# A hybrid stick-breaking / RWKV-7 layer on one core: the opening's loads, norm and gain spread rebuilt, V's projection called later, the sampled state update in full shape

## The chip, the core and the metric

One NeuronCore of a Trainium2 chip runs the whole layer in one launch. The metric is device time in microseconds (us). Engines are named as in the profile: PE (matmul), PEld (its weight loads), DVE (vector), ACT (scalar), POOL (GpSimd), SP (the queue that issues most DMAs).

## The reference

For 512 prompt tokens of one stream and 16 new tokens of each of 8 running streams (640 rows of width 1024, one layer), cut to what matters:

```python
h = rmsnorm(x, norm_g)                    # x * rsqrt(mean(x*x)) * norm_g
proj = h @ w_in                           # one projection: q,k,v,z_A | gates | r,k,v,w-lora,a-lora,z_B
o_a = stick_breaking_attention(q, k, v)   # 16 heads x 64
p_mix = p_b + mu_shift * (p_prev - p_b)   # token shift on the RWKV columns
S_t = S_{t-1} (diag(w_t) - kk_t^T (kk_t*a_t)) + v_t^T k_t ;  o_t = S_t r_t   # 16 heads x 64
y_a = (o_a * silu(z_a)) @ w_o_a ;  y_b = (groupnorm(o_b) + bonus) * silu(z_b) @ w_o_b
x + (sig(g_a)*y_a + sig(g_b)*y_b) @ w_out # then a final RMSNorm; k, v, shift rows and states go out too
```

## The kernel before

**Opening** (`start`, `late`). The 640 rows are five tiles x of 128 rows. Each is squared and summed on ACT (`square`), its 1/rms made by small DVE steps and a square root on ACT (`rstd`), scaled on DVE by 1/rms and by `gb`, the gain norm_g spread over all partitions (`scale`), transposed on PE into two banks, copied as fp32r into `xh` by ACT, with the rest `xl` taken by DVE (`put`). Tiles 3 and 4 lie in `x34`; `late` transposes them in the middle of the first product. `warm(n)` issues n idle products of a zero tile `wz`.

**Products** (`gemm_range`). A job is 128 columns of a projection: its weights `raw` come by DMA, ACT rounds them to `whi`, DVE takes the rest `wlo`, and PE adds, for eight k and two halves of the rows, xh·whi + xl·whi + xh·wlo: 48 products of some 320 columns. ps_g banks hold the results.

**Order.** The program is written out by a planner. `Driver.run` keeps generators (streams) and the main line of jobs; at each `yield` it looks at a model of the engines' clocks (`Clock`) and steps the first stream that the model calls ready, else the main line, which can also be held by a gate. Jobs come from three lists (`job`): `mixed` (R, K, V, in that order for each of 8 head pairs p, first come first served), `free` (q, k, v, z, gate A: the filling, spilled to DRAM as `sp`, and z_B after each V) and `later`. The head of `mixed` is called two jobs before it runs, when its `soon` is true or no filling is left; its gate can then still hold the main line.

**The recurrence of a pair.** `prep(p)` makes decay, keys and masks from R and K (its low-rank weights `wd` are split into `wh`, `wl`), `prep2` inverts small triangles on POOL, `samp` and `chain` run the steps, `sstate` (started from the first chain step) updates the eight sampled streams' states, `post` norms the result. V(p) writes over the buffer that `post(p-3)` still reads, so V's gate is `post(p-3)`. When the last post is done the attention streams open, with the remaining jobs as filling; then come the output products.

In `sstate` the tile `ux` holds, per group g of four streams, the last step's values masked by stream; products with `BKt` give the update, DVE adds the old state `S0T` into `sn`, POOL scales `sn`, PE transposes it.

Of the kernel before, what the change touches and what calls it, by code (L numbers as in the profile page):

```python
# [340 lines left out]
def body(tc, ins, outs, dbg=None):  # L341
# [157 lines left out]
    def gemm_range(i0, i1):  # L499
# [6 lines left out]
        for i in range(i0, i1):  # L506
# [59 lines left out]
    def start():  # L566
        x34 = pers.tile([128, 2, D], F32, tag="H", name="x34")
        srow = pers.tile([88, 3, 128], F32, tag="V", name="srow", bufs=3)
        with pool("start", bufs=1) as sp:
            xt = [sp.tile([128, D], F32, tag="x", name="x", bufs=3) for _ in range(3)]  # L570
            xt += [x34[:, 0], x34[:, 1]]

            def loadx(i):
                dma(out=xt[i], in_=ins["x_prompt"][0, i * 128:(i + 1) * 128, :] if i < 4 else
                    ins["x_sample"].rearrange("b t d -> (b t) d"))
            gb = sp.tile([128, D], F32, name="gb")
            wz = sp.tile([128, 512], BF16, name="wz")
            V.memset(wz, 0.0)
            psw = bank("g")

# [9 lines left out]
            dma(out=ident, in_=ins["consts"][:, 0:128])  # L590
            loadx(2)
            wload(0)
            loadx(3)
            loadx(4)
            prow = sp.tile([97, 128], F32, name="prow")
# [8 lines left out]
            dma(out=cst[:, 128:NC], in_=ins["consts"][:, 128:NC])  # L604
            sv = sp.tile([128, 5], F32, name="sv")
            sr = sp.tile([128, 5], F32, name="sr")
            st = sp.tile([128, 5], F32, name="st")
            junk = sp.tile([128, D], F32, name="junk")
# [4 lines left out]
            def rstd(i0, i1):  # L613
                c = slice(i0, i1)
# [8 lines left out]

            def pscale(i):
                G.tensor_scalar(out=xt[i], in0=xt[i], scalar1=sr[:, i:i + 1], scalar2=1.0, op0=ALU.mult, op1=ALU.mult)
                gtt(xt[i], xt[i], gb, ALU.mult)
# [84 lines left out]
    def rwkv_load(p):  # L711
        o = rw[p]
        wd = o["wd"] = tr.tile([128, 2, 128], F32, tag="wd", name="wd")
        for r, n in enumerate(("w2", "a2")):
            for half in range(2):
                dma(out=wd[RS[half], r, :], in_=ins[n][0, :, p * 128:(p + 1) * 128])

    def state_load(p):
        o = rw[p]
# [8 lines left out]
    def prep(p):  # L728
        yield flag("rkfree", p - 1) if p else flag("lat")
        o = rw[p]  # L730
        wd = o["wd"]
        yield [wd]
        wh = tr.tile([128, 2, 128], F32R, tag="wh", name="wh")
        wl = tr.tile([128, 2, 128], F32R, tag="wl", name="wl")
# [85 lines left out]
        rk = kkn  # L820
        stt(rk, R, pcol(RK, p), K, ALU.mult, ALU.mult)
        setf("rkfree", p)
        yield [H, BK]
# [270 lines left out]
    def sstate(p):  # L1094

        o = rw[p]
        X, BKt, S0T, wc = (o[n] for n in ("X", "BKt", "S0T", "wc"))
        psn = yield from take("b", X, hold=True)
        for g in range(2):
            uxs = [ch.tile([128, 4, 64], F32, tag="ux", name="ux", bufs=2) for _ in range(2)]  # L1100
            for h in range(2):
                gtt(uxs[h], X[:, 8 + g, h, :].unsqueeze(1).broadcast_to([128, 4, 64]),
                    cview["msk4"].unsqueeze(2).broadcast_to([128, 4, 64]), ALU.mult)
            yield uxs
# [3 lines left out]
        sn = ch.tile([128, 8, 64], F32, tag="sn", name="sn")  # L1108
        vtt(sn, psn.rearrange("p (b v) -> p b v", b=8), S0T, ALU.add)
        give(psn)  # L1110
        setf("schain", p)
# [15 lines left out]
    def post(p, S8):  # L1127
# [22 lines left out]
        tp(ps[0:64, 0:128], S8, ident)  # L1150
        so8 = ch.tile([64, 128], F32, tag="ux", name="so8", bufs=2)
        V.tensor_copy(so8, ps[0:64, 0:128])
# [269 lines left out]
    with tc.manual_schedule():  # L1422
# [91 lines left out]
        for p in range(NPAIR):  # L1514
# [224 lines left out]
        tr = tr_cm.__enter__()  # L1739
        G.memset(STG, 0.0)  # L1740
        for t in ABD:
            G.memset(t, 0.0)
        drv.run(program())
# [36 lines left out]
```

## Time and profile before

| what | value |
|---|---|
| median of 3 runs | 1173.54 us (1167.69 to 1175.17) |
| profiled execution | 1171.08 us, of which 1169.3 us span |
| granted PE clock over the span | 0.99 |
| DMA | 130.70 MB, mean 112 GB/s |

The span is what the trace covers; the execution is 1.78 us longer, and the profiled one lies 2.46 us under the median. The first 30 us are the opening, the recurrence with its jobs runs to about 775 us, the attention to about 1035 us, then come output products alone.

### The profile page before, as it was taken

To read this page: it belongs to the slowest core of one execution; us is meant where nothing else is said; L and a number is where in the kernel's file an instruction comes from. 1 tells how busy PE (TensorE), PEld (TensorE's weight loads), DVE (VectorE), ACT (ScalarE), POOL (GpSimd) and SP (SyncE) were. 2 spreads that over 40 slices of the span, in tenths; PEclk is the share of its full clock that TensorE was granted. 3 is DMA by queue.
4 is the path that set the end of the run, shared out by engine and by line. 5 is a ranking of instruction groups with operands and counts; after the bars stand their busy time and mean duration, and the time that the engine had idled before them with its cause. 6 is when DMAs were issued, how large, how long until landed. Compare 5 with 4: busy or idle time off the path is not lost. (4 is left out here: it accounts for less than half of the span.)

```text
span 1169.3 us, 25426 instructions
## 1 busy us (share of the span) xinstructions
PE 1111.5 (95%) x10050; PEld 1037.7 (89%) x10050; DVE 746.2 (64%) x1517; ACT 629.8 (54%) x1347; POOL 390.5 (33%) x605
## 2 busy tenths in 40 slices
PE   6999899989999999999899999999999989999997
PEld 4989899979989989889799899998888878899997
DVE  6485974847765867857767544337777688765424
ACT  5636357646666477466575556445555544522223
POOL 3033315125222243342342513034444454323302
PEclk9999999989999999999999999999999999999999
DMA  5222222213132232133132333369666676366312
GB/s 193 78 89 57 78 66 82 84 50 115 62 95 77 67 93 79 55 88 89 52 93 90 98 103 102 108 184 261 180 161 160 172 216 177 82 197 188 105 56 91
DMA packets 205294, 130.70 MB, mean 112 GB/s; under 512 B 78332, under 2 KB 184696, under 8 KB 205176
## 3 DMA queue, kind: packets, MB, share of 16 engines
q1 hardware_dynamic: 204888, 129.03, 37.8%
q8 instruction: 79, 1.29, 0.4%
q14 instruction: 39, 0.32, 0.1%
q0 software_dynamic: 288, 0.05, 0.0%
HBM read 97.70 MB, written 31.35 MB: 110 GB/s over the span
## 5 line engine op out<-in xcount | busy, mean ns | idle before, releaser
L213 PE MATMUL ps_g<-xh,whi 128*128 128x320 f32 (+1 forms) x1424 | 468.5, 329 | 1.7 <-ACT xh L213 1.3
L213 PE MATMUL ps_g<-xl,whi 128*128 128x320 f32 (+1 forms) x1424 | 443.5, 311 | 3.3 <-DVE xl L213 3.3
L213 PE MATMUL ps_g<-xh,wlo 128*128 128x320 f32 (+1 forms) x1424 | 443.0, 311 | 1.4 <-DVE wlo L213 1.4
L213 PEld LDWEIGHTS ps_g<-xh,whi 128*128 128x128 f32 x1424 | 271.4, 191 | 9.3 <-issue 3.0
L213 PEld LDWEIGHTS ps_g<-xl,whi 128*128 128x128 f32 x1424 | 270.9, 190 | 6.4 <-DVE xl L213 4.5
L213 PEld LDWEIGHTS ps_g<-xh,wlo 128*128 128x128 f32 x1424 | 270.0, 190 | 2.4 <-DVE wlo L213 2.4
L213 DVE TENSOR_TENSOR wlo<-raw,whi 128x1024 fp32r<-128x1024 f32 x97 | 123.6, 1274 | 69.6 <-ACT whi L213 69.0
L213 ACT ACTIVATE whi<-raw 128x1024 fp32r<-128x1024 f32 x97 | 102.7, 1059 | 48.6 <-DMA raw<-in_w_o_a_dram 28.6
L213 DVE TENSOR_TENSOR_SCAN kp<-kp,amsk 128x256 f32<-128x256 f32 (+3 forms) x80 | 73.6, 929 | 27.8 <-ACT kp L213 27.7
L213 POOL TENSOR_TENSOR bt<-bt,amsk 128x128 f32<-128x128 f32 x64 | 44.0, 691 | 124.3 <-ACT bt L213 81.5
L213 POOL TENSOR_TENSOR itmp<-INV 128x28 f32<-128x28 f32 (+6 forms) x112 | 47.0, 420 | 90.8 <-DVE INV L213 82.9
L213 ACT ACTIVATE kp<-ps_a 128x512 f32<-128x512 f32 (+3 forms) x72 | 33.1, 460 | 68.0 <-PE ps_a L213 42.2
L213 ACT ACTIVATE RH<-ps_b 128x128 f32<-128x128 f32 (+1 forms) x64 | 19.4, 302 | 77.8 <-PE ps_b L213 77.4
L213 ACT ACTIVATE sp<-ps_g 128x320 f32<-128x320 f32 x80 | 34.6, 437 | 45.9 <-PE ps_g L213 40.6
L213 ACT ACT_TABLE_LOAD x39 | 50.0, 1283 | 8.9 <-DVE BK L213 5.4
L213 DVE SCALAR_TENSOR_TENSOR X<-ps_b,wc,SW 64x64 f32<-64x64 f32 x96 | 26.7, 278 | 35.7 <-PE ps_b L213 34.9
L213 POOL TENSOR_TENSOR on<-on,V 128x640 f32<-128x640 f32 x8 | 12.4, 1550 | 108.9 <-ACT on L213 108.9
L213 DVE TENSOR_TENSOR bt<-bt,kp 128x511 f32<-128x511 f32 (+4 forms) x72 | 42.4, 588 | 7.7 <-POOL bt L213 0.3
L213 POOL TENSOR_TENSOR INV<-INV,itmp 128x28 f32<-128x28 f32 (+6 forms) x112 | 43.6, 390 | 8.8
L213 PE MATMUL ps_b<-cst,bt 128*128 128x128 f32 x192 | 33.5, 278 | 12.4 <-DVE bt L213 11.8
L213 PE MATMUL ps_g<-olo,mgh 128*128 128x256 f32 x160 | 45.0, 281 | 0.0
L213 PE MATMUL ps_g<-ohi,mgh 128*128 128x256 f32 x160 | 45.0, 281 | 0.0
(252 smaller groups left out, 2319.4 us busy)
## 6 DMA issues: line engine op xcount, KB each, us to landing
raw<-in_w_in_dram SPq DMA_DIRECT2D x81, 512.0 KB
q<-dr_q SPq DMA_DIRECT2D x32, 160.0 KB
Kr<-in_cache_sb_k_dram SPq DMA_DIRECT2D x16, 256.0 KB
Vp<-in_cache_sb_v_dram SPq DMA_DIRECT2D x16, 256.0 KB
raw<-in_w_o_b_dram SPq DMA_DIRECT2D x8, 512.0 KB
raw<-in_w_o_a_dram SPq DMA_DIRECT2D x8, 512.0 KB
oraw<-in_w_out_dram SPq DMA_DIRECT2D x4, 1024.0 KB
dr_zB<-zm SPq DMA_DIRECT2D x8, 320.0 KB
```

Of the source, the lines that this page charges most:

```text
L213: r = f(*a, **k)
```

## The change

- Opening: x and the other first loads are issued by SP and ACT in turn. norm_g comes as one row (`grow`) and PE spreads it: a column of ones times the row, two products of 512 columns, copied to `gb` by ACT. A square root on a dummy tile stands before them on ACT. Each tile is normed singly (before: 0; 1 and 2; 3 and 4). The low part of the first weights goes to POOL. The clearing of `STG` and of the two `AB` tiles on POOL comes in `late` (before: ahead of the jobs). Idle products: 6, 8, 4, 4, 4 (before 18, 6, 3).
- `gemm_range` yields after every k (before: every second).
- `rwkv_split(p+1)` splits the next pair's low-rank weights at the end of `prep(p)` (before: at the start of `prep(p+1)`).
- `sstate`: one product of 128x512 per group (before: two of 64x256 each), four DVE adds of 64x256 (before: one of 128x512), and the bank is not held over both groups.
- V(p) is called when `post(p-3)` is done (before: when `chain(p-3)` is).

```diff
@@ gemm_range
-                    if k % 2:
-                        yield
+                    yield
@@ start
+            ring = (nc.sync.dma_start, nc.scalar.dma_start)
             def loadx(i):
-                dma(out=xt[i], ...)
+                ring[i % 2](out=xt[i], ...)
+            V.memset(one, 1.0)
+            V.memset(sr, 1.0)
+            loadx(0)
+            ring[1](out=grow, in_=ins["norm_g"])
+            loadx(1)
+            ring[1](out=ident, in_=ins["consts"][:, 0:128])
+            loadx(2)
+            loadx(3)
+            wload(0)
+            loadx(4)
+            act(out=st, in_=sr, func=AF.Sqrt)
-            warm(18)
-            loadx(0)
-            dma(out=gb, in_=ins["norm_g"].partition_broadcast(128).rearrange("p o d -> p (o d)"))
-            loadx(1)
...
+            warm(6)
+            for hf in range(2):
+                ps = bank("g")
+                c = slice(hf * 512, hf * 512 + 512)
+                mm(ps, lhsT=one, rhs=grow[:, c], start=True, stop=True)
+                act(out=gb[:, c], in_=ps, func=AF.Copy)
+            warm(8)
...
             square(0)
-            rstd(0, 1)
+            rstd(0)
             scale(0)
             square(1)
-            square(2)
-            rstd(1, 3)
+            rstd(1)
             scale(1)
             put(0, xt[0], "ab")
-            warm(6)
+            warm(4)
+            square(2)
+            rstd(2)
+            scale(2)
             wsplit(0)
-            scale(2)
+            gtt(jobs[0].lo, jobs[0].raw, jobs[0].hi.bitcast(F32), ALU.subtract)
             put(1, xt[1], "ab")
-            warm(3)
-            wlow(0)
+            warm(4)
+            put(2, xt[2], "ab")
+            warm(4)
             square(3)
+            rstd(3)
+            scale(3)
             square(4)
-            put(2, xt[2], "ab")
-            warm(0)
-            rstd(3, 5)
+            rstd(4)
+            scale(4)
...
-            scale(3)
-            scale(4)
@@ late
+        for t in (STG, *ABD):
+            G.memset(t, 0.0)
@@ prep
-        yield [wd]
-        wh = ...; wl = ...
-        act(out=wh, in_=wd, func=AF.Copy)
-        yield [wh]
-        gtt(wl, wd, wh.bitcast(F32), ALU.subtract)
-        if p + 1 < NPAIR:
-            rwkv_load(p + 1)
+        if p == 0:
+            yield [o["wd"]]
+            rwkv_split(0)
...
+        if p + 1 < NPAIR:
+            rwkv_split(p + 1)
         setf("rkfree", p)
@@ sstate
+        sn = ch.tile([128, 8, 64], F32, tag="sn", name="sn")
         for g in range(2):
+            ux = ch.tile([128, 2, 4, 64], F32, tag="ux", name="ux")
             for h in range(2):
-                gtt(uxs[h], ...)
+                gtt(ux[:, h], ...)
-            for h in range(2):
-                mm(psn[RS[h], g * 256:(g + 1) * 256], lhsT=BKt[:, 8 + g, h * 64:(h + 1) * 64],
-                   rhs=uxs[h].rearrange("p b v -> p (b v)"), start=True, stop=True)
-        vtt(sn, psn.rearrange("p (b v) -> p b v", b=8), S0T, ALU.add)
+            ps = yield from take("b", ux)
+            mm(ps, lhsT=BKt[:, 8 + g, :], rhs=ux.rearrange("p h b v -> p (h b v)"), start=True, stop=True)
+            for h in range(2):
+                vtt(sn[RS[h], c], pv[RS[h], h], S0T[RS[h], c], ALU.add)
+            yield []
@@ program, jobs of pair p
-                g2, s2 = [("post", p - 3)], s2 + [("chain", p - 3)]
+                g2, s2 = [("post", p - 3)], s2 + [("post", p - 3)]
```

Where the instructions stand. First ACT, from its first instruction to the second tile's square root; `junk` is the square, `sr` the root, `x_105` the tile `x34`. Before:

```order
L213 ACT_TABLE_LOAD
L213 ACTIVATE junk,sv<-x 128x1024
L213 ACT_TABLE_LOAD
L213 ACTIVATE sr<-sv 128x1
L213 ACTIVATE junk,sv<-x 128x1024 x2
L213 ACTIVATE sr<-sv 128x2
```

and after:

```order
L589 DMA grow<-in_norm_g_dram 1x1024
L575 DMA x<-in_x_prompt_dram 128x1024
L591 DMA cst<-in_consts_dram 128x128
L575 DMA x_105<-in_x_prompt_dram 128x1024
L213 ACT_TABLE_LOAD
L213 ACTIVATE st<-sr 128x5
L213 ACTIVATE gb<-ps_g 128x512 x2
L213 ACTIVATE junk,sv<-x 128x1024
L213 ACTIVATE sr<-sv 128x1
L213 ACTIVATE junk,sv<-x 128x1024
L213 ACTIVATE sr<-sv 128x1
```

The second table load is gone from between the first square and its root; four DMA issues and two copies from PE's banks now stand ahead of the first square.

Next POOL, from the last small parameter load on; the name AB_102, AB_103 are the two AB tiles. Before:

```order
L600 DMA prow<-in_r_k_dram 8x128
L213 MEMSET STG 128x1024
L213 MEMSET AB_102 128x2560
L213 MEMSET AB_103 128x2560
L213 ISA
L213 TENSOR_TENSOR wl<-wd,wh 128x256
```

and after:

```order
L616 DMA prow<-in_r_k_dram 8x128
L213 ISA
L213 TENSOR_TENSOR wlo<-raw,whi 128x1024
L213 MEMSET STG 128x1024
L213 MEMSET AB_102 128x2560
L213 MEMSET AB_103 128x2560
L213 TENSOR_TENSOR wl<-wd,wh 128x256
```

The clearing now stands behind the first weights' low part, and so after the third tile's scale.

Last PE, at the sampled update of pair 1, just ahead of V of pair 3 (whose jobs are the rows that write ps_g). Before:

```order
L213 MATMUL ps_g<-xh,wlo 128x320
L213 MATMUL ps_b<-ux,BKt 64x256 x2
L213 MATMUL ps_b<-X,BKt 128x128
L213 MATMUL ps_c<-X,AB_103 128x128
L213 MATMUL ps_a<-H,BK 128x128 x8
L213 MATMUL ps_b<-ux,BKt 64x256 x2
L213 MATMUL ps_b<-cst,sn 128x128 x4
L213 MATMUL ps_g<-xh,whi 128x320
```

and after (the transposes of sn follow 39 rows further down, behind 27 more job products):

```order
L213 MATMUL ps_g<-xh,wlo 128x320
L213 MATMUL ps_b<-ux,BKt 128x512
L213 MATMUL ps_a<-lat,wh 128x320
L213 MATMUL ps_a<-lat,wl 128x320
L213 MATMUL ps_a<-lat,wh 128x320
L213 MATMUL ps_a<-lat,wl 128x320
L213 MATMUL ps_b<-RH,AB_103 128x128
L213 MATMUL ps_g<-xh,whi 128x320
```

Job products now stand between the update and the transposes of its result, where before none did. V of pair 3 is the 26th job of the program (before the 23rd), V of pair 7 the 53rd (before the 51st).

## Rows read from the trace of the kernel before

**Rows 1.** The page: busy time by engine; a group (busy us, mean ns).

```profile
PE 1111.5 (95%) x10050; PEld 1037.7 (89%) x10050; DVE 746.2 (64%) x1517; ACT 629.8 (54%) x1347; POOL 390.5 (33%) x605
...
L213 POOL TENSOR_TENSOR on<-on,V 128x640 f32<-128x640 f32 x8 | 12.4, 1550 | 108.9 <-ACT on L213 108.9
```

**Rows 2.** PE's waits, whole span: us in total, times, longest.

```profile
PE ps_b L213 <- POOL sn L213: 8.9, 5, 3.9
...
PE ps_a L213 <- POOL wl L213: 3.3, 3, 2.7
```

**Rows 3.** Timeline of the opening: start us, duration us, instruction, count, idle before.

```profile
1.19 6.66 PE L584 MATMUL ps_g<-wz 128*128 128x512 bf16 x18 [1.19 <-DVE wz L213]
...
4.29 1.06 ACT L213 ACTIVATE junk<-x 128x1024 f32<-128x1024 f32 x1 [2.27 <-DMA x<-in_x_prompt_dram]
...
5.46 1.28 ACT L213 ACT_TABLE_LOAD   x1
...
7.96 1.28 DVE L213 SCALAR_TENSOR_TENSOR x<-x,sr,gb 128x1024 f32<-128x1024 f32 x1
8.22 4.42 POOL L213 MEMSET AB<- 128x2560 f32 x2
...
10.23 1.46 PE L584 MATMUL ps_g<-wz 128*128 128x512 bf16 x6
...
11.48 1.20 DVE L213 TENSOR_SCALAR sv<-sv 128x2 f32<-128x2 f32 x1 [2.23 <-ACT junk L213]
...
22.60 2.47 DVE L213 SCALAR_TENSOR_TENSOR x<-x,sr,gb 128x1024 f32<-128x1024 f32 x2
...
27.88 0.68 DVE L213 TENSOR_TENSOR xl<-ps_a,xh 128x512 fp32r<-128x512 f32 x1
...
28.62 0.42 PE L213 MATMUL ps_g<-xl,whi 128*128 128x322 f32 x1 [0.53 <-DVE xl L213]
```

**Rows 4.** Busy us (count) of each engine from 20 to 25 us, then PE clock.

```profile
20.00:25.00 5.00, 4.63 (x22) 4.40 (x22) 4.53 (x12) 1.54 (x4) 0.00 (x0) 0.66 0.36 105
```

**Rows 5.** The same (PE, PEld, DVE, ACT, POOL) for three stretches without job products.

```profile
239.75:247.49 7.74, 3.82 (x35) 2.66 (x33) 4.38 (x10) 0.54 (x2) 2.32 (x5) 0.87 0.07 26
415.51:424.14 8.63, 7.26 (x48) 4.56 (x46) 5.09 (x9) 7.82 (x17) 7.43 (x6) 1.00 0.35 102
570.18:583.21 13.03, 10.10 (x62) 6.23 (x60) 9.68 (x21) 9.26 (x21) 9.78 (x11) 1.00 0.24 68
```

**Rows 6.** The same for 5 us behind the first stretch, and the 5 us after.

```profile
247.49:252.50 5.01, 5.01 (x19) 4.62 (x18) 1.00 (x5) 0.60 (x1) 0.00 (x0) 0.52 0.31 52
252.50:257.50 5.00, 5.00 (x42) 4.76 (x41) 1.61 (x4) 3.63 (x8) 0.00 (x0) 1.00 0.38 107
```

**Rows 7.** Timeline, PE and DVE: a sampled update, and a 64x256 step.

```profile
157.98 0.31 PE L213 MATMUL ps_g<-xh,wlo 128*128 128x320 f32 x1
158.22 0.65 PE L213 MATMUL ps_b<-ux,BKt 128*64 128x256 f32 x4
...
158.80 0.49 PE L213 MATMUL ps_b<-RH,AB 128*128 128x128 f32 x2
...
162.03 0.68 DVE L213 TENSOR_TENSOR sn<-ps_b,S0T 128x512 f32<-128x512 f32 x1
...
420.80 0.42 DVE L213 TENSOR_TENSOR AB<-ps_a,cst 64x256 f32<-64x256 f32 x1 [0.36 <-PE ps_a L213]
```

**Rows 8.** PE timeline: two fp32 products of 320 columns and what follows.

```profile
51.85 1.24 PE L213 MATMUL ps_a<-nrm,cst 128*128 128x320 f32 x4
...
52.69 0.55 PE L213 MATMUL ps_g<-xh,whi 128*128 128x322 f32 x1
```

**Rows 9.** Timeline: last post, last attention gate, last of the filling's results.

```profile
773.17 1.58 POOL L213 TENSOR_TENSOR zb<-zb,Oa 128x640 f32<-128x640 f32 x1
...
1015.22 2.08 POOL L213 TENSOR_TENSOR sg<-sg,sz 128x640 f32<-128x640 f32 x1 [1.04 <-PE ps_c L213]
...
1048.11 0.49 DVE L213 TENSOR_TENSOR m<-ps_g,m 128x320 f32<-128x320 f32 x1 [2.55 <-PE ps_g L213]
```

More of the change, by code (lines that the diff above doesn't have):

```diff
@@ L571, in start @@
             xt += [x34[:, 0], x34[:, 1]]
+            ring = (nc.sync.dma_start, nc.scalar.dma_start)
             def loadx(i):
-                dma(out=xt[i], in_=ins["x_prompt"][0, i * 128:(i + 1) * 128, :] if i < 4 else
-                    ins["x_sample"].rearrange("b t d -> (b t) d"))
+                ring[i % 2](out=xt[i], in_=ins["x_prompt"][0, i * 128:(i + 1) * 128, :] if i < 4 else
+                            ins["x_sample"].rearrange("b t d -> (b t) d"))
             gb = sp.tile([128, D], F32, name="gb")
+            grow = sp.tile([1, D], F32, name="grow")
+            one = sp.tile([1, 128], F32, name="one")
             wz = sp.tile([128, 512], BF16, name="wz")
+            sv = sp.tile([128, 5], F32, name="sv")
+            sr = sp.tile([128, 5], F32, name="sr")
+            st = sp.tile([128, 5], F32, name="st")
+            junk = sp.tile([128, D], F32, name="junk")
             V.memset(wz, 0.0)
+            V.memset(one, 1.0)
[9 more added lines that the diff above has]
+            act(out=st, in_=sr, func=AF.Sqrt)
             psw = bank("g")
@@ L584, in warm @@
                     nc.tensor.matmul(psw, lhsT=wz[:, 0:128], rhs=wz, start=True, stop=True)
-            warm(18)
-            loadx(0)
-            dma(out=gb, in_=ins["norm_g"].partition_broadcast(128).rearrange("p o d -> p (o d)"))
-            loadx(1)
[L590 to L594, printed above, removed]
+            warm(6)
[5 more added lines that the diff above has]
+            warm(8)
             prow = sp.tile([97, 128], F32, name="prow")
@@ L604, in start, with rstd @@
             dma(out=cst[:, 128:NC], in_=ins["consts"][:, 128:NC])
[L605 to L608, printed above, removed]
             def square(i):
                 act(out=junk, in_=xt[i], func=AF.Square, accum_out=sv[:, i:i + 1])
-            def rstd(i0, i1):
-                c = slice(i0, i1)
+            def rstd(i):
+                c = slice(i, i + 1)
                 V.tensor_scalar(out=sv[:, c], in0=sv[:, c], scalar1=1.0 / D, scalar2=EPS,
@@ L622, in scale @@
                 stt(xt[i], xt[i], sr[:, i:i + 1], gb, ALU.mult, ALU.mult)
-            def pscale(i):
-                G.tensor_scalar(out=xt[i], in0=xt[i], scalar1=sr[:, i:i + 1], scalar2=1.0, op0=ALU.mult, op1=ALU.mult)
-                gtt(xt[i], xt[i], gb, ALU.mult)
             square(0)
-            rstd(0, 1)
+            rstd(0)
             scale(0)
             square(1)
-            square(2)
-            rstd(1, 3)
+            rstd(1)
             scale(1)
             put(0, xt[0], "ab")
-            warm(6)
+            warm(4)
+            square(2)
+            rstd(2)
+            scale(2)
             wsplit(0)
-            scale(2)
+            gtt(jobs[0].lo, jobs[0].raw, jobs[0].hi.bitcast(F32), ALU.subtract)
             put(1, xt[1], "ab")
-            warm(3)
-            wlow(0)
+            warm(4)
+            put(2, xt[2], "ab")
+            warm(4)
             square(3)
+            rstd(3)
+            scale(3)
             square(4)
-            put(2, xt[2], "ab")
-            warm(0)
-            rstd(3, 5)
+            rstd(4)
+            scale(4)
             ps = bank("c")
@@ L716, in rwkv_load, with rwkv_split @@
                 dma(out=wd[RS[half], r, :], in_=ins[n][0, :, p * 128:(p + 1) * 128])
+    def rwkv_split(p):
+        o = rw[p]
+        wh = o["wh"] = tr.tile([128, 2, 128], F32R, tag="wh", name="wh")
+        wl = o["wl"] = tr.tile([128, 2, 128], F32R, tag="wl", name="wl")
+        act(out=wh, in_=o["wd"], func=AF.Copy)
+        gtt(wl, o["wd"], wh.bitcast(F32), ALU.subtract)
+        if p + 1 < NPAIR:
+            rwkv_load(p + 1)
     def state_load(p):
@@ L730, in prep @@
         o = rw[p]
-        wd = o["wd"]
-        yield [wd]
-        wh = tr.tile([128, 2, 128], F32R, tag="wh", name="wh")
-        wl = tr.tile([128, 2, 128], F32R, tag="wl", name="wl")
-        act(out=wh, in_=wd, func=AF.Copy)
-        yield [wh]
-        gtt(wl, wd, wh.bitcast(F32), ALU.subtract)
-        if p + 1 < NPAIR:
-            rwkv_load(p + 1)
+        if p == 0:
+            yield [o["wd"]]
+            rwkv_split(0)
+        wh, wl = o["wh"], o["wl"]
         sg = tr.tile([128, T], F32, tag="sg", name="sg")
@@ L821, in prep @@
         stt(rk, R, pcol(RK, p), K, ALU.mult, ALU.mult)
+        if p + 1 < NPAIR:
+            rwkv_split(p + 1)
         setf("rkfree", p)
@@ L1097, in sstate @@
         X, BKt, S0T, wc = (o[n] for n in ("X", "BKt", "S0T", "wc"))
-        psn = yield from take("b", X, hold=True)
+        yield [X]
+        sn = ch.tile([128, 8, 64], F32, tag="sn", name="sn")
         for g in range(2):
-            uxs = [ch.tile([128, 4, 64], F32, tag="ux", name="ux", bufs=2) for _ in range(2)]
+            ux = ch.tile([128, 2, 4, 64], F32, tag="ux", name="ux")
             for h in range(2):
-                gtt(uxs[h], X[:, 8 + g, h, :].unsqueeze(1).broadcast_to([128, 4, 64]),
+                gtt(ux[:, h], X[:, 8 + g, h, :].unsqueeze(1).broadcast_to([128, 4, 64]),
                     cview["msk4"].unsqueeze(2).broadcast_to([128, 4, 64]), ALU.mult)
-            yield uxs
+            ps = yield from take("b", ux)
+            mm(ps, lhsT=BKt[:, 8 + g, :], rhs=ux.rearrange("p h b v -> p (h b v)"), start=True, stop=True)
+            pv = ps.rearrange("p (h b v) -> p h b v", h=2, b=4)
+            c = slice(4 * g, 4 * g + 4)
             for h in range(2):
-                mm(psn[RS[h], g * 256:(g + 1) * 256], lhsT=BKt[:, 8 + g, h * 64:(h + 1) * 64],
-                   rhs=uxs[h].rearrange("p b v -> p (b v)"), start=True, stop=True)
-        sn = ch.tile([128, 8, 64], F32, tag="sn", name="sn")
-        vtt(sn, psn.rearrange("p (b v) -> p b v", b=8), S0T, ALU.add)
-        give(psn)
+                vtt(sn[RS[h], c], pv[RS[h], h], S0T[RS[h], c], ALU.add)
+            yield []
         setf("schain", p)
@@ L1150, in post @@
         tp(ps[0:64, 0:128], S8, ident)
-        so8 = ch.tile([64, 128], F32, tag="ux", name="so8", bufs=2)
+        so8 = ch.tile([64, 128], F32, tag="ux", name="so8")
         V.tensor_copy(so8, ps[0:64, 0:128])
@@ L1739, in body @@
         tr = tr_cm.__enter__()
-        G.memset(STG, 0.0)
-        for t in ABD:
-            G.memset(t, 0.0)
         drv.run(program())
```

## Prediction

> **What bounds the kernel now.** I read the page's busy times first: PE is busy for 95% of the span and no other engine for over 64% [rows 1]. So PE's own work is the floor, and an edit gains only where PE stands still, runs at its lower clock, or is given less to do. The waits of PE come next [rows 2]: most of them end in DVE or POOL. Then two places in order of time. In the opening [rows 3] PE can't do real work before the rows are normed and transposed; the first half of job 0 runs by 20 us, but steady work starts only when tile 4's `xl` is there: the product at 28.62 waits for the piece that starts at 27.88. Everything behind is nearly gapless, so a microsecond here is a microsecond of the whole. The second place is three stretches of the recurrence in which PE has no job products at all [rows 5]. They lie just ahead of V of pairs 3, 5 and 7: V has been called, since its chain was done, its gate waits for a post, and the main line can't hand out filling. There the small steps of `chain`, `prep` and `sstate` stand behind one another with nothing between.
>
> **The opening.** Removed: the 512 KB spread of norm_g, one table load (1.28) between the first square and its root, and the 1.05 by which a DVE step of 0.15 took 1.20 while POOL cleared AB (the clearing that starts at 8.22 runs to 12.64) [rows 3]. Added: the spread by PE ahead of the first square in ACT's queue. Its price: six idle products at 0.37 each (18 took 6.66) from 1.19 end at 3.4. A product of two fp32 halves: two of 320 columns start at 51.85 and the next job's product at 52.69 [rows 8], 0.42 each, or 0.62 each by the 1.24 of their duration; times 512/320 that is 0.67 to 0.99, middle 0.83, at full clock. The later six idle products took 1.46, 0.24 each, against 0.37 of the first 18 [rows 3], so PE was mostly at its lower level (1.2 GHz) in the first 7 us, and the two products cost some 3.3 instead of 1.7. They end at 6.7, ACT's last copy (half of a 1.06 square) ends at some 7.4, and the first square starts then instead of at 4.29.
>
> From there I lay the tiles out one behind another. From a square's start to its scale it was 3.67 (4.29 to 7.96); without the table load 2.39, of which 1.33 comes behind the square. Scale 0 starts at 9.8. DVE keeps order, so the next tile's small steps stand behind this scale: 1.28 + 1.33 = 2.6 per tile, scale 1 at 12.4. Two `xl` pieces of tile 0 (0.68 each) lie ahead of tile 2's steps: scale 2 at 16.4, end 17.7; the four `xl` pieces of tiles 1 and 2 end at 20.4. That is about when job 0 started before: what the loads, the table and the clearing gave is spent on the late start. For tiles 3 and 4 two scales ran back to back from 22.60, to 25.07. Now tile 3's steps wait for its square (from about 19.8, so to 20.9), and 20.9 + 2 x 2.6 = 26.1: 1.0 later, because tile 4's small steps no longer share tile 3's. The six pieces behind them are unchanged.
>
> Two things on top. The clearing (4.42 for AB alone) now follows POOL's low part of the first weights (1.55 for 640 columns [rows 1], so 2.5 for 1024, from about 17) and falls on the steps of tiles 3 and 4: each may be held by 1.05 as before, 0 to 2.1. And PE is nearly idle between the end of job 0's first half and 28 us; before, a like pause left a granted clock of 0.66 from 20 to 25 us [rows 4]. That one lay on a half that was not last; now one would fall on work that is: 5 x 0.34 = 1.7. I take half of each: 1.0 + 1.05 + 0.85 = **+2.9**. The lower end is -1 (the spread at full clock, 1.7 earlier, no collision), the upper +5.
>
> A rule of the Trainium skill bears on the clearing. In this trace the small one-input step was stretched by it, while the scale at 7.96, with two tensor inputs, took 1.28 under it, and two with POOL idle 2.47 together, 1.24 each [rows 3]. The Trainium skill, GPSIMD Engine Reference, section Specifications, says that POOL shares SBUF interfaces with DVE, with contention for DVE instructions in a 2-port mode or with two SBUF inputs. By it the two late scales would be held as well; at 1.05 each (an estimate from this trace's step) the opening would be +5.0 instead of +2.9. The row on the scale speaks against that for a clearing.
>
> **V's call.** In the three stretches PE is busy for 21.2 of 29.4 us and its weight loads for 13.5 [rows 5]; in dense work loads fill 4.76 of 5.00 [rows 6]. What could be filled lies between the idle 8.2 and 15.9 (29.4 less 13.5). With V called only when its buffer is free, q, k, v, z and gate jobs stand there: the order shows job products between the sampled update and its transposes, where none were. I take the middle, **-12**; the low end of the gain is 4, if half of the idle time moves elsewhere. The first stretch also brings 5 us at a clock of 0.52 [rows 6], half of which is lost: **-2.3**. What pays: V and the R and K behind it come later, which is the slower rival below.
>
> **Low-rank weights.** PE's wait for `wl`, 3.3 in 3 [rows 2], goes, since the split now ends long before its user; 0.3 lies in a stretch already counted: **-3.0**, 0 if ACT is late next. The same DMAs are issued on SP a little earlier; nothing waits for them there.
>
> **Sampled update.** Two products of 64x256 stand between a job product's start at 157.98 and the next start at 158.80, 0.82 [rows 7]; less 0.13 for the job product (320 columns at 2.4 GHz) 0.69. One of 128x512 takes 0.67 to 0.99 by the bounds above, 0.83 in the middle: +0.14 for each of 16 groups, **+2.2** (0 to +5). DVE pays 4 x 0.42 for 0.68, 1.0 per pair, beside PE's work. Of PE's wait for `sn`, 8.9 in 5 [rows 2], the half outside the stretches stays: in some pairs of the new order the transposes still follow closely.
>
> **Yield at every k.** No instruction is added, but all later orders are drawn anew by a planner whose clock model made the waits that there are; a wait that it foresaw badly can come anywhere. I set **+4** for that (-2 to +9), nearest to the wait for `sn` outside the stretches, about half of the 8.9.
>
> **Sum.** 2.9 - 12 - 2.3 - 3.0 + 2.2 + 4 = -8.2 on 1171.08, so 1162.9 for an execution like the profiled one; that one lies 2.46 under its median, so the median to expect is **1165**.
>
> **Rivals.**
> - *More comes back.* All 15.9 of the stretches are filled, the new order brings no new wait, the product is cheap and the opening gains 1: -1 - 15.9 - 2.3 - 3.0 + 0 + 0 = -22, a median of 1151. For it: DVE, ACT and POOL have time to spare over the span. Against: in the second and third stretch ACT and POOL are busy for most of it, 17.1 and 17.2 of 21.7 us [rows 5], so part of the waiting is theirs, whoever fills PE.
> - *The stretches give nothing.* The gate was only where the small steps' latency showed; spread out, the same waits stand between job products. Then 2.9 - 3.0 + 2.2 = +2.1 without the two terms and with no new waits: 1176. For it: the busy rows just named. Against: in the first stretch ACT and POOL are busy for 2.9 of 7.7 us, and PE waits for one result.
> - *Slower: the chain becomes the bound.* R and K of the next pair can't pass V. V of pair 3 moves from the 23rd to the 26th job, V of pair 7 from the 51st to the 53rd. If a chain then stands waiting for its `prep`, the last post (end 774.8) comes later by up to three jobs, each 48 products of 0.13, with the small work between them some 30 us, and the attention with it; filling spent early is missing there. The last filling is consumed at 1048, after the last attention pair at 1017 [rows 9], so so 31 us are covered; it decides from there. With a delay of 45 (another job or two), 14 us stay open: 2.9 - 3.0 + 2.2 + 14 = +16.1, 1190. Against: before, V(3) had tens of us until its chain, since its gate opens on a post that precedes two other chains.
> - *The opening does the opposite of its aim.* Already in the sum; with all its upper ends it moves the forecast by +2.
>
> **How the numbers follow.** Forecast (1159 to 1171) 0.50, more back 0.20, nothing from the stretches 0.22, slower 0.08. The time is the forecast's, 1165. The range 1151 to 1179 reaches to both middle rivals and leaves out most of the slower one and the lower edge of the first. About 1% (11.7 us) is what a measurement of this kernel can tell from no change: below 1161.8 lies most of the first rival and a quarter of the forecast, 0.30; above 1185.3 the slower rival, 0.07; the rest, 0.63, is within.
>
> **What would show it.** In the new profile the first square should start near 7.4 and steady job products at 29 to 33 us; no stretch of over 5 us without job products should stand ahead of V of pairs 3, 5 and 7, and no `wl` among PE's waits; a sampled product should stand for 0.7 to 1.0; the last post should end by 775 or earlier. A first square by 5.5 would break the opening's term; new waits of over 10 us in the recurrence, or a later last post, the forecast.

## The result and the profile after

The changed kernel takes **1183.74 us** (median of 7 runs, 1181.71 to 1185.86) against 1173.54 us (by now 7 runs too, 1167.69 to 1176.98): a ratio of 1.0088, 95% interval 1.0071 to 1.0104. It is slower by 0.9%, clear of the noise, and lies above the predicted range of 1151 to 1179. Its profiled execution took 1183.07 us, 1181.3 us of it span. Two lines of its page, busy times and granted clock in 40 slices:

```profile
PE 1119.5 (95%) x10020; PEld 1043.3 (88%) x10021; DVE 766.1 (65%) x1554; ACT 630.9 (53%) x1351; POOL 402.2 (34%) x606
...
PEclk9999999999999999999999899999999999999999
```

Against [rows 1] PE is busy 8.0 us longer, and it is idle for 1181.3 - 1119.5 = 61.8 us where it was 1169.3 - 1111.5 = 57.8: +4.0. Those 12.0 us are the whole difference of the spans. The same split is used for every run below, since nothing else than PE's busy and idle time is in a span. Busy time also holds what the lower clock costs. By the clock that the traces record, PE ran at half speed (1.2 GHz) for 22.7 us of the span before and for 32.6 after (mean granted clock 0.990 and 0.986). At half speed a stretch loses at most half of its length, so up to 4.9 of the 8.0 us are the clock's.

**The opening.** The timeline of the changed kernel, rows of ACT, DVE, POOL and PE in order of time (start, duration, engine, line, operation, count, and in brackets the idle time ahead and what ended it):

```profile
5.98 0.60 ACT L213 ACTIVATE gb<-ps_g 128x512 f32<-128x512 f32 x1 [1.60 <-PE ps_g L213]
...
7.68 0.60 ACT L213 ACTIVATE gb<-ps_g 128x512 f32<-128x512 f32 x1 [1.11 <-PE ps_g L213]
8.18 1.05 ACT L213 ACTIVATE junk<-x 128x1024 f32<-128x1024 f32 x1
...
10.74 1.28 DVE L213 SCALAR_TENSOR_TENSOR x<-x,sr,gb 128x1024 f32<-128x1024 f32 x1
...
17.14 3.45 DVE L213 SCALAR_TENSOR_TENSOR x<-x,sr,gb 128x1024 f32<-128x1024 f32 x1
17.17 2.34 POOL L213 TENSOR_TENSOR wlo<-raw,whi 128x1024 fp32r<-128x1024 f32 x1 [9.65 <-ACT whi L213]
...
20.34 4.42 POOL L213 MEMSET AB<- 128x2560 f32 x2
...
23.55 0.15 DVE L213 TENSOR_SCALAR sv<-sv 128x1 f32<-128x1 f32 x1 [0.24 <-ACT junk L213]
24.94 1.29 DVE L213 SCALAR_TENSOR_TENSOR x<-x,sr,gb 128x1024 f32<-128x1024 f32 x1
27.53 1.28 DVE L213 SCALAR_TENSOR_TENSOR x<-x,sr,gb 128x1024 f32<-128x1024 f32 x1
...
31.99 0.41 PE L213 MATMUL ps_g<-xl,whi 128*128 128x322 f32 x1 [0.53 <-DVE xl L213]
```

The first square starts at 8.18 (before 4.29), because ACT's two copies of the gain stand ahead of it. Tile 2's scale takes 3.45 instead of 1.28 us: it starts as POOL begins the subtraction of the first weights. The later clearing (20.34 to 24.76) does not hold the small step at 23.55, and the scale at 24.94 starts when it is over. Steady products start at 31.99 instead of 28.62 [rows 3], and right behind stands a stretch at the lower clock, the first of three windows of the changed kernel (start and end; length; busy time of PE, PEld, DVE, ACT, POOL; granted clock; DMA):

```profile
32.00:36.50 4.50, 4.50 (x21) 4.49 (x22) 1.73 (x3) 0.39 (x1) 0.00 (x0) 0.62 0.01 4
...
646.83:654.59 7.76, 1.94 (x10) 1.11 (x8) 4.38 (x10) 3.41 (x8) 1.55 (x3) 0.73 0.11 42
650.50:657.50 7.00, 3.68 (x17) 3.64 (x18) 3.80 (x10) 1.28 (x3) 3.88 (x10) 0.52 0.06 9
```

**The recurrence.** The waits of PE in the changed kernel (operation waited with, releaser: us in total, times, longest):

```profile
PE ps_b L213 <- DVE bt L213: 13.0, 17, 1.9
PE ps_b L213 <- POOL sn L213: 12.0, 3, 5.8
...
PE ps_a L213 <- POOL wl L213: 2.7, 1, 2.7
PE ps_b L213 <- DVE X L213: 2.6, 4, 1.7
PE ps_a L213 <- DVE Y L213: 2.4, 3, 2.0
PE ps_a L213 <- POOL H L213: 2.2, 1, 2.2
```

The largest, for `bt`, is much as before (11.8 in 18). The stretches directly ahead of V are gone, but `sn` is waited for longer than in [rows 2], and `wl` is still there. Each of the three waits for `sn` makes a stretch without job products of its own, of 7.1, 5.6 and 7.4 us from 487.7, 570.5 and 647.1, and a filling job follows each of them. The longest wait, in the second window above, read over the engines:

```profile
646.80 1.55 ACT L213 ACTIVATE X<-ps_a 64x256 f32<-64x256 f32 x4
646.98 1.02 PE L213 MATMUL ps_b<-ux,BKt 128*128 128x512 f32 x2
...
648.83 1.06 ACT L213 ACTIVATE whi<-raw 128x1024 fp32r<-128x1024 f32 x1
649.92 1.23 DVE L213 TENSOR_TENSOR wlo<-raw,whi 128x1024 fp32r<-128x1024 f32 x1 [3.53 <-ACT whi L213]
651.78 0.86 DVE L213 TENSOR_TENSOR sn<-ps_b,S0T 64x256 f32<-64x256 f32 x2
652.72 1.04 POOL L213 TENSOR_TENSOR sn<-sn,wc 128x512 f32<-128x512 f32 x1 [7.51 <-DVE sn L213]
653.82 1.12 PE L213 MATMUL ps_b<-cst,sn 128*128 128x128 f32 x4 [5.82 <-POOL sn L213]
```

The product is done by 648, but the additions that read it stand on DVE behind `wlo`, DVE waits 3.53 us for ACT's `whi`, ACT is behind other copies, and the transposes of `sn` are the next thing in PE's order. No job product stands between: a stretch of the same kind as [rows 5], in another place, with its half-speed stretch behind it (0.52).

The last post starts 10.6 us earlier than in [rows 9]:

```profile
762.60 2.43 POOL L213 TENSOR_TENSOR zb<-zb,Oa 128x640 f32<-128x640 f32 x1
```

### The profile page after: what moved, and what is told of

The parts are those of the page before. It is cut to its first block, busy times and chain, and to the rows that moved or that the text cites. A ratio compares the mean times of both kernels' runs of the same rounds, so it can differ in the third digit from the quotient of the medians.

```text
span 1181.3 us, 25421 instructions
## 1 busy us (share of the span) xinstructions
PE 1119.5 (95%) x10020; PEld 1043.3 (88%) x10021; DVE 766.1 (65%) x1554; ACT 630.9 (53%) x1351; POOL 402.2 (34%) x606
## 5 line engine op out<-in xcount | busy, mean ns | idle before, releaser
L213 ACT ACTIVATE kp<-ps_a 128x512 f32<-128x512 f32 (+3 forms) x72 | 33.0, 459 | 67.2 <-PE ps_a L213 33.0
L213 POOL TENSOR_TENSOR ux<-X,cst 128x256 f32<-128x256 f32 x32 | 21.7, 700 | 94.4 <-DMA out_wkv_prompt_dram<-so 50.6
L213 DVE TENSOR_TENSOR bt<-bt,kp 128x511 f32<-128x511 f32 (+4 forms) x72 | 45.8, 636 | 8.1 <-DVE kp L213 0.5
```

The lines of the kernel that those rows point to most:

```text
L213: r = f(*a, **k)
```

## The experiments

**1. The parts alone, and the change less one part.** Four kernels are the one before with one part of the diff, four the changed one without that part. The parts are those of the diff above; a yield after every "product" in the texts below is one after every k, which is three products:

```diff
@@ opening (b_open; undone in a_open): start(), late() and the clearing, as in the diff of the change
@@ V's call (b_v; a_v)
-                g2, s2 = [("post", p - 3)], s2 + [("chain", p - 3)]
+                g2, s2 = [("post", p - 3)], s2 + [("post", p - 3)]
@@ sampled update (b_ss; a_ss): sstate() as in the diff of the change
-                mm(psn[RS[h], g * 256:(g + 1) * 256], lhsT=BKt[:, 8 + g, h * 64:(h + 1) * 64],
+            mm(ps, lhsT=BKt[:, 8 + g, :], rhs=ux.rearrange("p h b v -> p (h b v)"), start=True, stop=True)
@@ finer yield (b_yk; a_yk)
-                    if k % 2:
-                        yield
+                    yield
```

> The kernel before with the new opening alone (x on two queues, the gain spread by a product, tiles normed singly, the low part of the first weights and the clearing of the decay buffers in their new places). Theory 1, the lag of the opening is carried to the end: the third scaling is held to about 3.4 us beside the subtraction on GpSimd, the second job ends some 5 us later than before, and the time is 1173.5 + 5 = 1178.5 (1176 to 1181). Theory 2, a lag of the first 40 us is taken up by waits that shrink later: within 2 us of before, 1172 to 1176.

Measured: 1178.18 us against 1172.70, ratio 1.0035 (1.0012 to 1.0058). Theory 1: the lag is carried to the end.

> The kernel before with V's call alone changed (its products may be begun early only once the pair three back has been posted). Theory 1, the call removes the three stretches without products of jobs (7.7, 8.6 and 13.0 us) and nothing takes their place: 1160 to 1166. Theory 2, the planner only moves the empty time: the wait for the updated sampled state or another one of the chain takes the place of the stretches, and the time is 1171 to 1177. Theory 3, the call itself costs, because products of jobs that used to stand between steps of the chain now come later: 1178 or more.

Measured: **1192.21 us**, 1.0167 (1.0138 to 1.0195): theory 3. The last post comes 21.6 us later than before, and here filling runs out: PE waits for the attention's output in the output products.

```profile
794.75 2.44 POOL L213 TENSOR_TENSOR zb<-zb,Oa 128x640 f32<-128x640 f32 x1
...
1057.25 0.64 PE L213 MATMUL ps_g<-oAl,whi 128*128 128x320 f32 x1 [2.05 <-DVE oAl L213]
1063.66 0.41 PE L213 MATMUL ps_g<-oAh,whi 128*128 128x320 f32 x1 [3.10 <-POOL oAh L213]
```

Of the three stretches of [rows 5] the call removes the second and the third. The first stands unchanged, half-speed time behind it included. First PE's timeline in the kernel before, at the end of that stretch:

```profile
239.60 0.31 PE L213 MATMUL ps_g<-xh,wlo 128*128 128x320 f32 x1
...
242.15 0.65 PE L213 MATMUL ps_b<-ux,BKt 128*64 128x256 f32 x4
246.72 1.11 PE L213 MATMUL ps_b<-cst,sn 128*128 128x128 f32 x4 [3.92 <-POOL sn L213]
247.49 0.61 PE L213 MATMUL ps_g<-xh,whi 128*128 128x320 f32 x1
```

then the same place with V's call alone, and its windows (as those above), the stretch and the 5 us behind it:

```profile
241.36 0.65 PE L213 MATMUL ps_b<-ux,BKt 128*64 128x256 f32 x4
245.93 1.12 PE L213 MATMUL ps_b<-cst,sn 128*128 128x128 f32 x4 [3.92 <-POOL sn L213]
...
239.06:246.70 7.64, 3.73 (x34) 2.65 (x33) 4.32 (x9) 0.54 (x2) 2.32 (x5) 0.87 0.06 22
246.70:251.70 5.00, 5.00 (x19) 4.61 (x18) 1.00 (x5) 0.60 (x1) 0.00 (x0) 0.51 0.32 52
```

In both kernels the stretch begins six products into a half of a filling job (the last of them at 239.60 before; the job's result goes to `sp`) and ends with a wait for `sn`. So filling was at hand there, with V's early call as without it; the planner had put the transposes of `sn` ahead of the job's other products. A new stretch of 7.8 us comes at 583.5, with a wait of 3.73 us for `sn`.

> The kernel before with the full-shape sampled update alone (two products of 128 x 512 for a pair in place of four narrower ones, four additions on VectorE in place of one, the place of the output in its own buffer). Theory 1, only the longer rows and additions count: some +0.6 us for a pair on TensorE and +1.0 on VectorE, of which the chain shows part: 1174 to 1179. Theory 2, the additions stand late in VectorE's order and TensorE waits for the updated state at its transposes, as after the whole change (12.0 us in 3 waits): 1180 to 1186. Theory 3, bank b comes free earlier and the chain gains: below 1172.

Measured: 1186.24 us, 1.0106 (1.0080 to 1.0131): just above the upper edge of theory 2, with PE waiting 4.06, 2.48, 2.96 and 2.47 us for `sn` at its four longest.

> The kernel before with a yield after every product of a job in place of every second one, alone. Theory 1, the finer interleaving shortens the waits of TensorE a little or moves them: 1169 to 1177. Theory 2, the finer steps let a step of the chain be placed before what it waits for is done, more short waits than 46: 1178 or more. Theory 3, it fills the stretches without products of jobs: 1168 or less.

Measured: 1169.05 us, 0.9959 (0.9942 to 0.9976), with the last post 26 us earlier: the lower edge of theory 1.

> The changed kernel with the opening of the kernel before. If the opening's lag is carried to the end, as the run of the opening alone says (5.5 us by medians), 1183.7 - 5 = 1179 (1176 to 1181). If the lag is taken up later, within 2 us of 1184.

Measured: 1178.84 us, so the opening costs 4.9 us of the whole by medians, and 4.3 when each kernel is taken against the kernel before of its own comparison. Alone it cost 5.5.

> The changed kernel with V's call of the kernel before. Alone, V's call cost 19.5 us. If prices add, this is 1164 (1160 to 1168). If the finer yield keeps the chain early, so that V's call does its harm only without it, it is 1180 to 1190, and the recurrence's last post stays near 763.

Measured: 1193.99 us. Without V's call the changed kernel is 10 us *slower*, with the last post at 771 instead of 763. Both expectations missed.

> The changed kernel with the sampled update of the kernel before (four narrower products and one addition). Alone, the full-shape update cost 13 us. If that is its own price, this is 1171 (1167 to 1175), and the waits for the updated state at its transposes (12.0 us in 3) go. If most of the 13 us came from the order that the planner drew around it, 1178 to 1186.

Measured: 1191.26 us. The wait for `sn` shrank as foreseen (its longest is 2.73), and the kernel became 7.5 us slower all the same. Both expectations missed.

> The changed kernel with a yield after every second product again. Alone, the yield after every product gained 3.7 us. If prices add, this is 1187 to 1190. If the finer yield is what pays back V's call (which cost 19.5 us alone and not in the whole change), it is 1195 to 1210, with the recurrence's last post at 780 or later. If the finer yield harms once V's call is made, 1180 or less.

Measured: 1213.26 us. The finer yield does pay back more than it gained alone, as the second expectation has it, and the price is above even its range; the last post is at 814, and output products wait for `oAl` and `oAh` as in the run of V's call alone.

What follows: of the parts tried, only the opening has about one price, alone and in the whole. V's call and the sampled update change sign with what is beside them, and the finer yield goes from -3.7 alone to -29.5 in the whole. The opening is also the only one of them that leaves the later order alone: compared without buffer numbers, PE's order of some 6245 rows shows 13 lines of difference to that of before, with V's call alone 1477.

**2. The order alone, and two pieces of the opening.** One order that the planner writes out is called a draw from here on.

```diff
b_n1, b_n3 (kernel before, Driver.run)
-  if at <= now + 0.02 and (best is None ...
+  if at <= now + 0.10 and (best is None ...      # b_n3: now + 0.0
a_low (changed kernel, start)
-  gtt(jobs[0].lo, jobs[0].raw, jobs[0].hi.bitcast(F32), ALU.subtract)
+  vtt(jobs[0].lo, jobs[0].raw, jobs[0].hi.bitcast(F32), ALU.subtract)
a_gblow (a_low and)
-  ring[1](out=grow, in_=ins["norm_g"])           # with its two products and copies
+  ring[1](out=gb, in_=ins["norm_g"].partition_broadcast(128)...)
```

> A control: the kernel before with the planner's slack (how far ahead of what its model calls ready a step may be placed) 0.10 instead of 0.02 us. The same instructions in another order, none of the parts of the change. If a redrawn order by itself moves the time no more than a measurement can tell, 1169 to 1177, and the prices of the single parts (+13 and +20 us) are their own. If redrawing alone costs, as theory: 1178 or more.

Measured: **1185.72 us** against 1172.87, 1.0129 (1.0104 to 1.0154).

> A second control: the kernel before with the planner's slack 0 instead of 0.02 us. The same reading: 1169 to 1177 if a redrawn order is neutral, 1178 or more (or 1165 or less) if the order alone moves the time as much as the parts do.

Measured: 1177.97 us against 1172.87, 1.0051 (1.0033 to 1.0068).

Both controls do the work of the kernel before and take up no part of the change (PE's order shows 1830 and 1593 lines of difference), and cost 12.9 and 5.1 us. The first has PE busy for 1115.3 of 1181.4 us; its idle time is 66.1 us, 8.3 more than before, although it waits for `sn` less than before did. Its waits of PE:

```profile
PE ps_b L213 <- DVE bt L213: 11.6, 16, 1.6
PE ps_g L213 <- DVE xl L213: 6.1, 5, 4.8
PE ps_b L213 <- POOL sn L213: 5.7, 5, 1.8
...
PE ps_b L213 <- DVE AB L213: 3.0, 2, 1.8
PE ps_b L213 <- DVE X L213: 2.9, 3, 2.2
```

So the waits of a redrawn order are other ones, each too small to name as a cause. In the second control PE's idle time is only 1.5 us more than before; there PE's busy time grew by 6.4, with 39.8 us at half speed where it was 22.7. Both controls change a setting of the planner, so it is not excluded that another slack than 0.02 costs something by itself.

> The changed kernel with one instruction of the opening on another engine: the low part of the first weights is taken by VectorE instead of GpSimd (TensorE's order stays word for word the same). If the third scaling took 3.45 us instead of 1.28 because GpSimd read two tensors beside it, it takes 1.2 to 1.4 now, the second half of the first job begins 1 to 2 us earlier and the time is 1181 to 1183. If the scaling is long for another reason (its tile, the gain's fresh copy), it stays at 3.4 and the time is 1184 to 1186, the subtraction on VectorE added.

Measured: 1182.09 us, 1.6 less than the change by medians, and 1.0 less when each is taken against the kernel before of its own comparison. Timeline of that kernel:

```profile
17.11 1.28 DVE L213 SCALAR_TENSOR_TENSOR x<-x,sr,gb 128x1024 f32<-128x1024 f32 x1
18.31 1.22 DVE L213 TENSOR_TENSOR wlo<-raw,whi 128x1024 fp32r<-128x1024 f32 x1
...
30.27 0.42 PE L213 MATMUL ps_g<-xl,whi 128*128 128x322 f32 x1 [0.53 <-DVE xl L213]
```

With the subtraction off POOL the scale is back at 1.28, and steady products start 1.72 earlier than in the changed kernel.

> As the run with the low part on VectorE, and the gain comes spread by a DMA as in the kernel before, with no products and no copies on ScalarE ahead of the first squaring. If the late first squaring (8.2 instead of 4.3 us) is what the opening loses, the first scaling starts near 8 instead of 10.7, steady products start at 28 to 29.5 and the time is 1179 to 1181. If the loads on two queues then come later because of the 512 KB of the spread, no gain against the run with the low part on VectorE alone.

Measured: 1181.66 us. Timeline of that kernel:

```profile
8.79 1.28 DVE L213 SCALAR_TENSOR_TENSOR x<-x,sr,gb 128x1024 f32<-128x1024 f32 x1
...
28.75 0.42 PE L213 MATMUL ps_g<-xl,whi 128*128 128x322 f32 x1 [0.53 <-DVE xl L213]
```

Steady products start 1.52 earlier still, at 28.75, within 0.13 of the kernel before. The time follows by 0.4 only, and lies above the expected 1179 to 1181. Part of the reason shows in the granted clock: this execution has half-speed stretches at 82, 137 and 884 us that the run with the low part on VectorE hasn't, in an order that is the same but for the opening. In all PE is at half speed for 46.0 us here and for 32.3 there, by one profiled execution of each.

**3. The parts in a second and third order, and two parts together.** V's call, the finer yield, the sampled update and the whole change with the slack of 0.10; the finer yield with the slack 0; the finer yield with V's call at 0.02. The edits are those shown, combined.

> V's call alone, drawn with the slack of 0.10 us. It is compared with the kernel before at that slack, 1185.7. If V's call costs by itself what it cost alone (19.5 us, the recurrence's last post 22 us later), 1205 with the last post near 770 (that draw's was at 747). If the 19.5 us were those of one unlucky order, anywhere from 1170 to 1195; and if the call gains what the prediction said, 1171 to 1178.

Measured: 1179.50 us, 6.2 *less* than its control. The last post is at 767.4 against that control's 747.5, so V's call again delays the recurrence by 20 us, and the time falls.

> The finer yield alone, drawn with the slack of 0.10 us, against 1185.7. If the yield gains by itself, 1182 or less with the last post before 747. If its 3.7 us were the draw, anywhere from 1168 to 1190, and the last post need not be earlier.

Measured: 1180.20 us, 5.5 less than its control, the last post unmoved (748.1).

> The full-shape sampled update alone, drawn with the slack of 0.10 us, against 1185.7. If the 13 us that it cost alone are its own (longer rows, later additions), 1195 to 1200. If they were the redrawn order's, 1172 to 1192, on either side of 1185.7.

Measured: 1186.70 us, 1.0 more than its control: not the 13.4 of the first order.

> The whole change, drawn with the slack of 0.10 us, against 1183.7 for the change and 1185.7 for the kernel before at that slack. If the change is worth its own +10 us whatever the order, 1196. If only the opening's 5 us are its own and the rest is the order, 1175 to 1200, around 1185.7 + 5.

Measured: 1203.16 us, 17.4 more than its control and above both expectations.

> The kernel before with the finer yield and V's call, without the other parts. The finer yield alone took 1169.1 with the last post at 750 us; V's call alone cost 19.5 us in one draw and gained 6 in another. If V's call gains by filling the stretches where the finer yield has brought the chain early, 1155 to 1166 and a version faster than both kernels. If V's call has no price that shows through the redrawn order, 1165 to 1185.

Measured: **1167.47 us** against 1174.14, 0.9949 (0.9930 to 0.9967): the fastest kernel of the study, ahead of both kernels, but by half a per cent, 6.7 us, short of the 1166 that the first theory asked for. It is one order among others: it doesn't show that the two parts gain by themselves.

> The finer yield alone in a third draw (slack 0), against the control at that slack, 1178.0. It gained 3.7 and 5.5 us in the other two draws. If that gain is the yield's own, 1171 to 1175 with the last post earlier than that control's 778 us. If it was the draws, anywhere from 1168 to 1190.

Measured: 1180.74 us, 2.8 more than its control. So the finer yield has no steady gain by itself: -3.7, -5.5 and +2.8 in three draws.

All orders that carry the opening of the kernel before, and an order other than its own, by the median less that of the kernel before in the same comparison; PE's times are those of the profiled run, and "half speed" is PE's time at its lower clock, in us of the span:

| kernel | against before, us | PE busy | PE idle | half speed | last post |
|---|---|---|---|---|---|
| before | 0 | 1111.5 | 57.8 | 22.7 | 773.2 |
| yield + V's call | -6.7 | 1111.5 | 56.5 | 22.3 | 748.7 |
| yield | -3.7 | 1113.9 | 55.2 | 29.9 | 746.8 |
| slack 0 | +5.1 | 1117.9 | 59.3 | 39.8 | 778.5 |
| whole less opening | +5.9 | 1116.1 | 63.1 | 36.4 | 759.2 |
| V's call, slack 0.10 | +6.2 | 1116.7 | 60.4 | 44.2 | 767.4 |
| yield, slack 0 | +6.6 | 1115.9 | 64.0 | 39.6 | 766.7 |
| yield, slack 0.10 | +6.9 | 1111.8 | 64.9 | 27.6 | 748.1 |
| slack 0.10 | +12.9 | 1115.3 | 66.1 | 35.5 | 747.5 |
| sampled update, slack 0.10 | +13.4 | 1114.2 | 67.2 | 31.9 | 753.9 |
| sampled update | +13.5 | 1120.1 | 64.0 | 47.8 | 774.3 |
| V's call | +19.5 | 1118.4 | 69.3 | 45.3 | 794.8 |

Nine of eleven redrawn orders are slower than the order of the kernel before; the mean of all eleven is +7.2 us (the sum of the column, 79.6, by 11). Only two of the eleven, the controls, carry no part of the change, so this mean is not the price of redrawing alone. The slower orders lose in two ways: all nine have PE idle for longer than before, and all nine have it at half speed for longer, up to 47.8 us against 22.7; how much of each differs from order to order. The last post doesn't rank the times: 747.5 stands beside +12.9 and 773.2 beside 0.

## Why the prediction was wrong, point by point

- **The step that failed is V's call, -12 and -2.3.** The prediction took the three stretches [rows 5] for one thing: V called, its gate shut, no filling to hand out. That holds for the second and the third, which lie between a finished job and V and go with the call. It doesn't hold for the first, which lies inside a filling job, waits 3.92 us for `sn` and stands unchanged with V's call alone. So 3.9 of the 8.2 idle us, and the half-speed stretch behind, were out of the call's reach. In place of the other two a stretch of 7.8 us comes with V's call alone, and three of 5.6 to 7.4 in the changed kernel, each with a wait for `sn`. PE's idle time from the first steady products to the end of the last post is 25.8 us before, 30.0 with V's call alone and 27.5 in the changed kernel: nothing of the gain is left. This is the mechanism of the second rival (the stretches give nothing); its 1176 had no term for the redrawn order and an opening 2 us too cheap.
- **V's call has no one price.** Against the kernel that differs only by it, it gave +19.5, -6.2, -10.2 (in the whole) and -1.6 (beside the yield), by medians, where the kernel before itself moved between 1172.7 and 1174.1 from one comparison to the next: no price of its own shows through the draws. The gain was booked in the place where it was read, while the whole order was drawn anew.
- **The price of a redrawn order, +4 (-2 to +9), was not too far off in its middle, but its range was too narrow.** The prediction took the waits of the kernel before as a sample of what any order would have. Orders with no part of the change cost +5.1 and +12.9, and six of the eleven lie outside -2 to +9. They lose by waits and by half-speed time; for this term the prediction counted waits alone. Which choices of the planner make an order fast or slow was not traced further; that stays open.
- **The opening, +2.9 (-1 to +5).** Measured +4.9 in the whole (+4.3 by the comparison's own kernel before) and +5.5 alone, about its upper end. The chain was laid out rightly: 2.6 us per tile (24.94, 27.53), a later first square, no gain left. Three sizes were off. The first square came at 8.18, not 7.4, +0.8. The half-clock stretch came in full, 1.7 where half was booked. And a term was missing: the subtraction moved to POOL beside tile 2's scale, 3.45 - 1.28 = 2.17; taken off POOL, the kernel gained 1.6 us by medians. The clearing's 0 to 2.1, of which half was booked, did not come. The step that took 1.20 in [rows 3] worked on 128x2, for two tiles together; the new steps work on 128x1, and such a step took 0.15 beside a clearing, at 7.58 in the kernel before and at 23.55 in the changed one. Whether the shape decides it was not tested.
- **The rule on POOL and DVE.** Tile 2's scale, with two SBUF tensors, took 3.45 us beside POOL's two-tensor subtraction and 1.28 with it gone; the scale at 7.96 in [rows 3] took 1.28 beside POOL's clearing. The Trainium skill, GPSIMD Engine Reference, section Specifications, states contention for DVE instructions with two SBUF inputs; the trace agrees beside POOL's TENSOR_TENSOR and shows no contention beside its MEMSET. The prediction weighed the rule against a clearing alone and did not carry it to the subtraction that the same diff moves to POOL.
- **Low-rank weights, -3.0.** Failed. The split waits on the same point as before: `prep(p+1)` was held until `rkfree(p)`, and the new place is the line ahead of `rkfree(p)`. In both kernels the subtraction that makes `wl` then stands on POOL behind four products for `H`, which end at 78.22 before and at 84.10 after. PE's wait was 2.74 before and is 2.68 (85.62). No run took this part alone.
- **Sampled update, +2.2.** The product itself was sized well: two passes stand from 642.91 to 643.78, 0.87, against 0.83 foreseen. Most of the 13.5 us that the part cost alone is not its own: at the second slack it cost 1.0, and the change without it was 7.5 us slower.
- **The slower rival**, the chain as the bound, shows its delay of the last post where V's call stands alone (+21.6, and +19.9 at the slack of 0.10), but it decided only where output products came to wait for the attention: V's call alone, and the change without the finer yield (1213.26). In the changed kernel the last post is earlier, and the rival did not happen.
- **The sum.** Opening +4.9, the rest +5.9 (the whole less the opening, against before), together +10.8 where +10.2 was measured and -8.2 forecast. The gains -12, -2.3 and -3.0 did not come; without them the prediction's own sum for the rest is 2.2 + 4 = +6.2. That this meets +5.9 is in part luck, since the eleven orders spread over 26 us. Of the +5.9 nothing can be put to a single part, since controls without any part cost as much.

## What to carry to other kernels

Where a planner or scheduler writes out the order, first measure a control that redraws the order and changes nothing; an edit of a few microseconds inside such a program can't be judged, or forecast, below the spread of those controls. Here nine of eleven new orders lost time against the one that there was, so an edit that redraws the order was likely to start with a loss; why the first order was a good one is not on record. The one edit that left the order alone, this opening, kept about the same price alone and in the whole. And before a gap is put down to a gate, look at what stands in the order just before and behind it: a gap inside a filling job has another cause. A wait removed in one place is only worth its length if the engine's busy and idle time over the whole span say so, and busy time has to be read together with the granted clock.

## What the runs showed of the hardware that was not expected

A scale of 128x1024 on DVE took 3.45 us where it started together with a 2.34 us subtraction on POOL: it ended some 1.1 us after POOL, and alone it takes 1.28, so it hardly advanced beside it. The same 3.45 (3.44 to 3.46) stands in all six kernels that have this subtraction there. A scale that ran beside a clearing on POOL (7.96 in the kernel before) lost nothing by it (1.28). The half-speed stretches of PE fall differently in kernels with the same order but for the opening: the run with the gain by DMA had three of them, at 82, 137 and 884 us, that its neighbour had not, and most of 1.5 us won in the opening was not in its time.
